# Attention values in full fp32, two heads in two 64-column tiles, and row sums added outside TensorE

## The chip, the cores and the metric

The kernel runs on one core of one Trainium2 chip. The metric is the time of one execution on the device in microseconds; the median over runs is compared.

## What is computed

One layer of a streaming encoder: a normalisation and one input projection, then three groups of heads on the projected columns (forgetting attention with 6 heads of 64, an RWKV-7 recurrence with 6 heads, cross-attention of 4 heads into 256 memory tokens), gates, one output projection and the residual. There are 2048 prompt tokens and eight sample streams of 16 tokens with 512 cached keys each; all is fp32. What the change touches is the softmax attention of the prompt, forgetting and memory:

```python
s = jnp.einsum('bqhd,bkhd->bhqk', q, k) * (HEAD_DIM ** -0.5)
s = s + jnp.transpose(cq, (0, 2, 1))[..., :, None] - jnp.transpose(ck, (0, 2, 1))[..., None, :]
s = jnp.where(kpos[None, :] <= qpos[:, None], s, jnp.finfo(jnp.float32).min)
p = jax.nn.softmax(s, axis=-1)
o = jnp.einsum('bhqk,bkhd->bqhd', p, v)
...
o = jnp.concatenate([o_f * jax.nn.silu(g_f), o_r * jax.nn.silu(g_r), o_m * jax.nn.silu(g_m)], axis=-1)
y = x + o @ w_out
```

## The kernel before

The program has two parts. The first, to about 1128 us, projects the input in four blocks of 512 tokens and runs the recurrence; queries, keys, values and gates go to DRAM. The second part holds the attention, the sample streams and the output projection.

Large products are done in a reduced-width form of fp32 (`F32R`): an operand is split into a high and a low part, and three matmuls (high-high, high-low, low-high) replace a full one. The splits are made by ScalarE (copy of the high part) and by GpSimd or VectorE (subtraction).

Attention works in units. A unit is a pair of heads `hp` (three pairs forgetting, two pairs memory) and a block of 512 queries `qb` (four). Forgetting units go over `4 * qb + 4` key tiles of 128, memory units over two. In the last four tiles of a forgetting unit the first columns are masked, so that widths of 512, 384, 256 and 128 queries remain. `queries` loads and splits the queries and takes row maxima from products of keys and queries (tile `pm`, reduced on VectorE). `attend` (from line 1138) does the rest, one key tile `kt` and one head `h` at a time, first all tiles of head 0, then of head 1:

- `scores` (line 1145): two matmuls into `pS` (two buffers), for masked tiles an addition on VectorE, the exponential on ScalarE into `P` (line 1154, two buffers), its high part `Ph` on ScalarE (line 1157), its low part `Pl` on GpSimd (`PLE`, line 61 of the helpers).
- `values` (line 1161), three steps (`LAG`) later: three matmuls into `po`, a PSUM tile of its own for each head with one buffer for forgetting units. The weights are the value tiles `vt` with a column of ones, 65 wide, so that row 64 of `po` is the row sum.
- at the last key tile three ScalarE copies take `po` to `ob` and the row sum; the row sums go to DRAM.
- `sums` (line 1204) reads them back as 32 x 32, takes reciprocals times 0.5, writes them to DRAM and reads them broadcast into `rb`; `out` multiplies `ob` by `rb` (VectorE) and by the gate (GpSimd) and stores it. The last forgetting unit has `ending` instead: one-row products spread the sums in `pd`.

`values_in` (line 1015) loads the values of 512 keys, fills `vt` with ones on GpSimd and splits the values on ScalarE and VectorE. `fox_keys` and `mem_keys` call it and make the split keys `K`.

Beside the forgetting units run memory units, sample streams and output projections (`py`, six to fifteen matmuls each, added on VectorE). The steps are emitted in a mix by their place in the sequence, and then `_arrange` orders all instructions of every engine anew: a list scheduler with a cost for each kind of instruction, due times and the buffers of each tile tries 18 orders and keeps the best by its own estimate. It takes neighbouring full fp32 matmuls that use less than the whole array as one unbroken run. It also knows which pools of the second part lie in the same SBUF bytes as pools of the first, and starts a tile only when those pools are done. The first keys `K` lie in pool `k0`, today in the bytes of pool `rw`; the pool behind that, `xs`, holds the normalised input `xk`.

## Time and profile before

| what | value |
|---|---|
| median of 3 runs | 1784.49 us (1782.93 to 1788.72) |
| span of the profiled execution, the only time given for it | 1786.9 us |
| granted TensorE clock, mean | 0.978 |
| HBM read, written | 210.15 MB, 90.28 MB |

The page has one line for the busy time of each engine. PE is TensorE's matmuls, PEld its weight loads, which run beside matmuls; DVE is VectorE, ACT ScalarE, POOL GpSimd, SP the queue that issues DMAs. The ends of matmuls are modelled, so that a matmul's duration includes about 0.17 us of the array's latency, which the next one overlaps: what a matmul costs in a stream is read from one start to the next. A full fp32 matmul stands in the trace as two records, a matmul in the reduced form as one. A row of a group gives the busy time in us, the mean in ns of one instruction, the engine's idle time before them and what ended it.

### The profile page before, as it was taken

How to read it: one execution, taken by the hardware profiler on the slowest of the kernel's cores; microseconds unless marked ns; L12 is line 12 of the kernel's file. 1: busy time of each engine (PE TensorE's matmuls, PEld its weight loads, DVE VectorE, ACT ScalarE, POOL GpSimd, SP SyncE). 2: the span in 40 equal slices, each digit the busy share in tenths (PEclk: the TensorE clock that was granted, in tenths of full speed). 3: DMA queues.
4: the chain of work that ended last, by engine and by line, in shares of the span. 5: the costliest groups of instructions: out<-in, count | busy, mean ns of one | idle time of the engine just before them, and what ended most of it. 6: DMA issues, size and time to landing. Idle time of an engine off the chain costs nothing.

```text
span 1786.9 us, 40906 instructions
## 1 busy us (share of the span) xinstructions
PE 1679.5 (94%) x16243; PEld 1347.0 (75%) x16243; DVE 980.2 (55%) x2310; ACT 897.2 (50%) x1783; POOL 808.7 (45%) x824
## 2 busy tenths in 40 slices
PE   4989999999899999999899999799999999989998
PEld 3989988787887688887688888576766666667776
DVE  6755554573444574345574372776545865676214
ACT  5434243434143523234323344688788777886552
POOL 4555452232312243132132143477687566766552
PEclk9999999999999999999899999799999899999999
DMA  7755764654645764655535654544445853344432
GB/s 207 276 185 174 224 196 143 206 188 137 201 143 150 245 194 145 193 167 176 169 113 166 190 169 154 156 127 139 156 149 172 271 207 110 103 152 158 155 111 107
DMA packets 236314, 303.11 MB, mean 170 GB/s; under 512 B 81594, under 2 KB 185976, under 8 KB 220250
## 3 DMA queue, kind: packets, MB, share of 16 engines
q1 hardware_dynamic: 236122, 300.49, 52.2%
q8 instruction: 128, 2.10, 0.5%
q14 instruction: 64, 0.52, 0.1%
HBM read 210.15 MB, written 90.28 MB: 168 GB/s over the span
## 4 chain that ended last, share of the span: by engine, by line
PE 51%; DMA 11%; DVE 6%; ACT 5%; POOL 3%; issue 2%; SPq 1%; DVEq 0%; POOLq 0%; ACTq 0%
PE pjd L58 12%; PE py L58 8%; PE po L58 7%; PE pjt L58 6%; PE pS L58 5%; PE pm L58 2%; DMA w<-w_d 1%; DMA xd<-inv_d 1%; POOL Pl L61 1%; PE sc L58 1%; ACT P L1154 1%; PE pz L58 1%; PE pa L58 1%; PE gr L58 1%; DMA AR<-sp_d 1%
## 5 line engine op out<-in xcount | busy, mean ns | idle before, releaser
L58 PE MATMUL pjd<-xk,w 128*128 128x512 f32 (+5 forms) x2280 | 537.8, 377 | 18.7 <-DMA w<-w_d 4.6
L58 PEld LDWEIGHTS pjd<-xk,w 128*128 128x128 f32 (+1 forms) x2280 | 385.8, 191 | 84.6 <-issue 7.8
L61 POOL TENSOR_TENSOR Pl<-P,Ph 128x512 fp32r<-128x512 f32 (+3 forms) x272 | 317.4, 1177 | 173.2 <-ACT Ph L1157 116.7
L58 PE MATMUL pjt<-w,xk 128*128 128x256 f32 x2040 | 295.5, 291 | 3.0 <-DVE xssg L64 1.7
L58 PEld LDWEIGHTS pjt<-w,xk 128*128 128x128 f32 x2040 | 267.8, 193 | 13.6 <-issue 3.9
L58 PE MATMUL py<-W,oh 128*128 128x512 f32 x816 | 239.1, 397 | 0.4 <-ACT Q L1126 0.2
L1154 ACT ACTIVATE P<-pS,NB 128x512 f32<-128x512 f32 x240 | 147.4, 623 | 88.8 <-PE pS L58 36.0
L58 PEld LDWEIGHTS py<-W,oh 128*128 128x128 f32 x816 | 149.9, 188 | 38.7 <-issue 0.8
L58 PE MATMUL pS<-Q,K 128*128 128x512 f32 (+1 forms) x480 | 154.7, 392 | 6.5 <-ACT P L1154 5.3
L58 PE MATMUL po<-Ph,vt 128*65 128x512 f32 x480 | 151.4, 370 | 4.2 <-ACT ob L1180 2.1
L1157 ACT CAST Ph<-P 128x512 fp32r<-128x512 f32 (+3 forms) x272 | 150.4, 565 | 9.1 <-PE po L58 4.5
L58 PEld LDWEIGHTS pS<-Q,K 128*128 128x128 f32 x480 | 85.5, 194 | 42.9 <-ACT P L1154 24.5
L1098 DVE TENSOR_REDUCE mx<-pm 128x1 f32<-128x512 f32 x144 | 95.2, 683 | 28.4 <-PE pm L58 27.3
L61 POOL TENSOR_TENSOR nr<-nr,mhalf 128x8 f32<-128x8 f32 (+2 forms) x43 | 61.7, 1435 | 98.7 <-DVE nr L67 89.2
L61 POOL TENSOR_TENSOR w<-wraw,w 128x1024 fp32r<-128x1024 f32 (+1 forms) x34 | 81.4, 2400 | 50.1 <-ACT w L202 44.8
L58 PE MATMUL pm<-K,Q 128*128 128x512 f32 (+3 forms) x240 | 92.8, 404 | 10.8 <-DVE mx L1095 5.2
L58 PE MATMUL po<-Pl,vt 128*65 128x512 f32 x240 | 89.1, 372 | 3.6 <-POOL Pl L61 3.5
L58 PEld LDWEIGHTS po<-Ph,vt 128*65 128x65 f32 x480 | 64.5, 137 | 33.2 <-ACT ob L1180 3.2
L61 DVE TENSOR_TENSOR xo<-py,xo 128x512 f32<-128x512 f32 x68 | 46.1, 686 | 75.3 <-PE py L58 74.9
L61 DVE TENSOR_TENSOR ytmp<-yt 64x14 f32<-64x14 f32 (+9 forms) x210 | 52.4, 249 | 42.0 <-DMA yt<-ld 37.4
L58 PEld LDWEIGHTS pm<-K,Q 128*128 128x128 f32 x240 | 47.2, 200 | 31.2 <-DVE mx L1095 7.9
L721 ACT COPY qk<-pjt 128x512 f32<-128x512 f32 (+1 forms) x47 | 26.1, 563 | 70.1 <-PE pjt L58 69.8
(404 smaller groups left out, 2820.0 us busy)
## 6 DMA issues: line engine op xcount, KB each, us to landing
w<-w_d SPq DMA_DIRECT2D x84, 1024.0 KB
w_d<-w SPq DMA_DIRECT2D x28, 1024.0 KB
y_d<-xo SPq DMA_DIRECT2D x21, 512.0 KB
wraw<-in_w_in SPq DMA_DIRECT2D x36, 256.0 KB
xo<-in_x SPq DMA_DIRECT2D x17, 512.0 KB
xo<-y_d SPq DMA_DIRECT2D x17, 512.0 KB
xt<-in_x SPq DMA_DIRECT2D x24, 256.0 KB
xraw<-in_xT SPq DMA_DIRECT2D x24, 256.0 KB
```

Source lines behind the costliest of these rows:

```text
L58: PE.matmul(out, lhsT, rhs, start=start, stop=stop, skip_group_check=True)
L61: e.tensor_tensor(out=out, in0=a, in1=b, op=op)
L721: S.copy(o_, out)
L1098: V.tensor_reduce(out=to, in_=pm[:, :n], op=MAX, axis=AX.X)
L1154: S.activation(P_[:, c0:], pS[:, c0:], AF.Exp, bias=NB[:, qb, 2 * hp + h, kt:kt + 1] if fox else 0.0)
L1157: S.copy(Ph[:, c0:], P_[:, c0:])
```

## The change

Values are kept in plain fp32 as they are loaded, without the column of ones and without a split. `P` is used as it is, also in fp32. Each head has one matmul per key tile, 64 columns wide; both heads write one `po`, head 0 in partitions 0 to 63 and head 1 in 64 to 127, and alternate. The steps are now groups of up to four key tiles of both heads (`GRP`); the values of a group are issued one group later (`LAG` = 1). `P` has 15 buffers, the tiles `Ph`, `Pl` and `rs` go. Row sums: from the second key tile on, GpSimd or VectorE adds `P` to a tile `z` for each head (two buffers for a pair), on VectorE for every third tile (`ZE`). `sums` then transposes `z` in blocks of 32 x 32, reduces it, adds across the four partition blocks with a matmul against a matrix of twos, and takes the reciprocal. One copy takes `po` to `ob`.

```diff
+ZE = "GGV"
-PMB, PSB, PB, HB, LB, LAG, NKB, BIG, POB, PTB = 2, 2, 2, 5, 5, 3, 4, 7, 1, 3
-PL = "G"
+PMB, PSB, PB, ZB, GRP, LAG, NKB, BIG, POB, PTB = 2, 2, 15, 2, 4, 1, 4, 7, 1, 3
...
+        twos = c2t("twos", [128, 128])
+        for j in range(4):
+            jj = slice(32 * j, 32 * j + 32)
+            ts(V, twos[jj].rearrange("p (a b) -> p a b", b=32), ident[jj, jj].unsqueeze(1).to_broadcast([32, 4, 32]), 2.0, None,
+               M, ALU.bypass)
...
-        def values_in(vt, vsrc, nt):
-            t_ = c2.tile([128, 4, 2, 64], F32, tag="tok", name="vtok", bufs=3)[:, :nt]
-            SY.dma_start(t_, vsrc.rearrange("(t p) (h d) -> p t h d", p=128, d=64))
-            G.memset(vt[:, 0:130 * nt].bitcast(F32), 1.0)
-            v1 = vt[:, 0:130 * nt].rearrange("p (t h d) -> p t h d", h=2, d=65)
-            v2 = vt[:, 130 * nt:258 * nt].rearrange("p (t h d) -> p t h d", h=2, d=64)
-            S.copy(v1[:, :, :, 0:64], t_)
-            tt(V, v2, t_, v1[:, :, :, 0:64].bitcast(F32), SUB)
-            return v1, v2
+        def values_in(vt, vsrc):
+            SY.dma_start(vt, vsrc.rearrange("(t p) (h d) -> p t h d", p=128, d=64))
+            return vt
...
-                vt = kp.tile([128, 1032], F32R, tag="vt", name="vt", bufs=NKB)
-                U["vt"].append(values_in(vt, v_d[gs, cs], 4))
+                vt = kp.tile([128, 4, 2, 64], F32, tag="vt", name="vt", bufs=NKB)
+                U["vt"].append(values_in(vt, v_d[gs, cs]))
...
-                P_ = lp.tile([128, 512], F32, tag="P", name="P", bufs=PB)
+                P_ = P[kt, h] = lp.tile([128, 512], F32, tag="P", name="P", bufs=PB)
                 S.activation(P_[:, c0:], pS[:, c0:], AF.Exp, bias=NB[:, qb, 2 * hp + h, kt:kt + 1] if fox else 0.0)
-                Ph = lp.tile([128, 512], F32R, tag="Ph", name="Ph", bufs=HB)
-                Pl = lp.tile([128, 512], F32R, tag="Pl", name="Pl", bufs=LB)
-                S.copy(Ph[:, c0:], P_[:, c0:])
-                tt(PLE[kt % len(PLE)], Pl[:, c0:], P_[:, c0:], Ph[:, c0:].bitcast(F32), SUB)
-                P[kt, h] = Ph, Pl
...
-                mm(po[h][0:65, c0:], v1, Ph[:, c0:], start=kt == 0, stop=False)
-                mm(po[h][0:64, c0:], v2, Ph[:, c0:], start=False, stop=False)
-                mm(po[h][0:65, c0:], v1, Pl[:, c0:], start=False, stop=kt == last - 1)
...
+                if kt == 1:
+                    if not h:
+                        R["z"] = lp.tile([128, 2, 512], F32, tag="z", name="z", bufs=ZB)
+                    if c0:
+                        G.tensor_copy(R["z"][:, h, :c0], P[0, h][:, :c0])
+                    tt(G, R["z"][:, h, c0:], P[0, h][:, c0:], P_[:, c0:], A_)
+                elif kt:
+                    tt(V if ZE[kt % len(ZE)] == "V" else G, R["z"][:, h, c0:], R["z"][:, h, c0:], P_[:, c0:], A_)
+
+            def values(kts):
+                if kts[0] == 0:
+                    R["po"] = (qc if fox else qa).tile([128, 512], F32, tag="po" if fox else "pt", name="po", bufs=POB if fox else PTB)
+                po = R["po"]
+                for kt in kts:
+                    c0 = c0_(kt)
+                    for h in range(2):
+                        mm(po[64 * h:64 * h + 64, c0:], U["vt"][kt // 4][:, kt % 4, h, :], P[kt, h][:, c0:],
+                           start=kt == 0, stop=kt == last - 1)
+                if kts[-1] == last - 1:
+                    R["ob"] = lt.tile([128, 512], F32, tag="ob", name="ob")
+                    S.copy(R["ob"], po)
+                    if dst is None:
+                        R["pd"] = qa.tile([128, 512], F32, tag="pt", bufs=PTB, name="pd")
+                        for h in range(2):
+                            mm(R["pd"][64 * h:64 * h + 64], one1.to_broadcast([128, 64]), R["z"][:, h])
...
             def sums():
+                rb = R["rb"] = lt.tile([128, 512], F32, tag="rb2", name="rb2", bufs=1)
+                zs = wk.tile([128, 32], F32, tag="zs", name="zs")
+                for h in range(2):
+                    V.transpose(rb, R["z"][:, h])
+                    V.tensor_reduce(out=zs[:, 16 * h:16 * h + 16], in_=rb.rearrange("p (a b) -> p a b", b=32), op=A_, axis=AX.X)
+                pz = qa.tile([128, 512], F32, tag="pt", bufs=PTB, name="pz")
+                mm(pz[:, 0:32], twos, zs)
+                rc = wk.tile([32, 2, 32], F32, tag="rc", name="rc")
+                V.reciprocal(rc[:, 0], pz[0:32, 0:32])
+                V.transpose(rc[:, 1], rc[:, 0])
                 rd = dt("rd", [2, 512], bufs=2)
-                rc = wk.tile([32, 32], F32, tag="rc", name="rc")
-                SY.dma_start(rc, R["sd"].rearrange("h (a b) -> (h a) b", b=32))
-                V.reciprocal(rc, rc)
-                ts(V, rc, rc, 0.5, None, M, ALU.bypass)
-                SY.dma_start(rd.rearrange("h (a b) -> (h a) b", b=32), rc)
-                R["rb"] = lt.tile([128, 512], F32, tag="rb2", name="rb2", bufs=1)
+                SY.dma_start(rd.rearrange("h (a b) -> (h a) b", b=32), rc[:, 1])
```

## Rows read from the trace of the kernel before

**Rows 1.** The page: its first line and part 1, the busy time of each engine with its share of the span and its instructions.

```profile
span 1786.9 us, 40906 instructions
...
PE 1679.5 (94%) x16243; PEld 1347.0 (75%) x16243; DVE 980.2 (55%) x2310; ACT 897.2 (50%) x1783; POOL 808.7 (45%) x824
```

**Rows 2.** Busy time of each engine in four stretches of the second part (start and end, length; then PE, PEld, DVE, ACT and POOL with their instructions, the granted clock, the DMA engines' share and GB/s).

```profile
1128.00:1179.00 51.00, 42.07 (x171) 29.04 (x171) 45.48 (x103) 39.46 (x77) 26.98 (x35) 0.77 0.52 165
1179.00:1382.00 203.00, 197.15 (x942) 141.02 (x940) 118.60 (x238) 170.57 (x310) 157.19 (x152) 1.00 0.46 145
1382.00:1585.00 203.00, 190.10 (x1379) 129.85 (x1380) 137.06 (x354) 163.97 (x318) 135.08 (x143) 0.96 0.51 172
1585.00:1787.00 202.00, 193.29 (x870) 144.75 (x868) 82.48 (x146) 99.36 (x172) 105.87 (x91) 1.00 0.39 136
```

**Rows 3.** Groups of PE from 1128 us to the end, different shapes apart: one of the three value matmuls of each step by its width, and the small full fp32 products of the sample units (two records each).

```profile
L58 PE MATMUL po<-Pl,vt 128*65 128x512 f32 x168 | 68.2, 406 | 1.8 <-POOL Pl L61 1.8
...
L58 PE MATMUL po<-Pl,Km 128*65 128x512 f32 x32 | 12.7, 396 | 1.0 <-POOL Pl L61 1.0
...
L58 PE MATMUL po<-Pl,vt 128*65 128x384 f32 x24 | 8.4, 348 | 1.7 <-POOL Pl L61 1.7
...
L58 PE MATMUL po<-Pl,vt 128*65 128x256 f32 x24 | 7.0, 292 | 0.0
L58 PE MATMUL po<-Pl,vt 128*65 128x128 f32 x24 | 5.7, 239 | 0.1
...
L58 PE MATMUL pN<-sD,one 128*128 128x128 f32 x12 | 3.1, 341 | 0.0
```

**Rows 4.** Timeline of PE near 1170 us (start, length of the merged piece, count): the three value matmuls of one step and what follows.

```profile
1169.79 0.62 PE L58 MATMUL po<-Ph,vt 128*65 128x512 f32 x2
1170.25 0.39 PE L58 MATMUL po<-Pl,vt 128*65 128x512 f32 x1
1170.48 0.40 PE L58 MATMUL pr<-idr,turnm 128*64 128x128 f32 x4
```

**Rows 5.** Timelines of PE: four full fp32 products in four 32-column tiles of the array in a sample unit, first in a window that holds the first four of their eight records only, then in one that holds all; then two such products in two 64-column tiles with 128 moving columns.

```profile
1432.69 0.40 PE L58 MATMUL pm<-K,Q 128*128 128x512 f32 x1
1433.02 0.64 PE L58 MATMUL pS<-sB,sD 128*32 128x512 f32 x4
...
1433.02 1.06 PE L58 MATMUL pS<-sB,sD 128*32 128x512 f32 x8
1434.02 0.50 PE L58 MATMUL pS<-Q,K 128*128 128x512 f32 x1
...
1417.68 0.44 PE L58 MATMUL po<-sD,sC 128*64 128x128 f32 x4 [0.23 <-ACT sD L1301]
```

**Rows 6.** Groups of ScalarE over the whole span: the copies of `P`, the exponentials of forgetting units, and one of the three closing copies.

```profile
L1157 ACT CAST Ph<-P 128x512 fp32r<-128x512 f32 (+3 forms) x272 | 150.4, 565 | 9.1 <-PE po L58 4.5
L1154 ACT ACTIVATE P<-pS,NB 128x512 f32<-128x512 f32 x240 | 147.4, 623 | 88.8 <-PE pS L58 36.0 <-DVE pS L61 32.9 <-POOL Pl L61 13.6
...
L1177 ACT COPY ob<-po 64x512 f32<-64x512 f32 x20 | 11.5, 578 | 0.4
```

**Rows 7.** Groups of GpSimd from 1128 us to the end, different shapes apart: the subtractions.

```profile
L61 POOL TENSOR_TENSOR Pl<-P,Ph 128x512 fp32r<-128x512 f32 x200 | 261.3, 1317 | 108.2 <-ACT Ph L1157 76.4 <-issue 14.1 <-PE pm L58 6.9
...
L61 POOL TENSOR_TENSOR Pl<-P,Ph 128x384 fp32r<-128x384 f32 x24 | 25.6, 1067 | 27.0 <-ACT Ph L1157 12.5 <-DMA y_d<-xo 5.4 <-PE po L58 3.5
...
L61 POOL TENSOR_TENSOR Pl<-P,Ph 128x256 fp32r<-128x256 f32 x24 | 18.1, 756 | 14.8 <-ACT Ph L1157 13.9 <-POOL Qm L1083 0.7
L61 POOL TENSOR_TENSOR Pl<-P,Ph 128x128 fp32r<-128x128 f32 x24 | 13.2, 548 | 23.2 <-ACT Ph L1157 13.9 <-PE pm L58 3.3 <-PE pS L58 3.1
```

**Rows 8.** Who waited for whom from 1140 us to the end (us in total, times, longest us): PE and its weight loads behind the exponential and behind the subtraction.

```profile
PEld pS L58 <- ACT P L1154: 29.3, 72, 1.8
...
PEld po L58 <- POOL Pl L61: 8.4, 13, 1.8
...
PE pS L58 <- ACT P L1154: 6.1, 11, 1.5
...
PE po L58 <- POOL Pl L61: 4.5, 5, 1.5
```

**Rows 9.** Instructions on the keys `K` and on the normalised input `xk` (duration in ns at least, median and at most; first and last start), and the first product of keys on PE's timeline.

```profile
L1004 POOL MEMSET K<- x24: 519/520/523, 1119.1 to 1612.0; 64x512 f32 x24
...
L58 PE MATMUL pjd<-xk,w x2280: 274/389/798, 19.2 to 1125.1; 128*128 128x512 f32 x105, 128*128 128x256 f32 x41, 128*128 128x384 f32 x32, 128*70 128x512 f32 x8
...
1126.64 0.30 PE L58 MATMUL pm<-K,Q 128*128 128x128 f32 x1 [1.13 <-POOL vt L1018]
```

**Rows 10.** VectorE: groups from 1128 us to the end (a maximum, an addition with one operand in PSUM, a product of two SBUF operands, the subtraction for the values, the scaling of the reciprocals), and the transposes of 128 x 256 at line 479 of the first part.

```profile
L1098 DVE TENSOR_REDUCE mx<-pm 128x1 f32<-128x512 f32 x144 | 95.2, 683 | 28.4 <-PE pm L58 27.3
L61 DVE TENSOR_TENSOR xo<-py,xo 128x512 f32<-128x512 f32 x68 | 46.1, 686 | 75.3 <-PE py L58 74.9
...
L61 DVE TENSOR_TENSOR ob<-ob,rb 128x512 f32<-128x512 f32 x19 | 17.4, 918 | 19.2 <-DMA rb<-rd 16.7 <-DMA ot<-o_d 2.0 <-issue 0.4
...
L61 DVE TENSOR_TENSOR vt<-vtok,vt 128x512 fp32r<-128x512 f32 x12 | 9.0, 751 | 4.8 <-ACT vt L1021 4.8
...
L67 DVE TENSOR_SCALAR rc<-rc 32x32 f32<-32x32 f32 x19 | 8.6, 452 | 0.4
...
L479 DVE STREAM_TRANSPOSE x<-xd x12: 445/446/447, 124.5 to 1079.3; 128x256 f32<-128x256 f32 x12
```

**Rows 11.** Busy time in the third stretch of the instructions on `Pl` alone (PE, PEld, POOL with their counts, clock, DMA share, GB/s).

```profile
1382.00:1585.00 203.00, 36.36 (x96) 13.39 (x96) 109.41 (x97) 0.96 0.51 172
```

More of the change, by code (lines that the diff above doesn't have):

```diff
@@ L979 @@
         taken = [0, 0]
-        PLE = [{"V": V, "G": G}[x] for x in PL]
         cl = lt.tile([48, 512], F32, tag="ob", name="cl")
@@ L1050, in step @@
                 m = big("Km", F32R)
[L1051 removed]
+                vt = m[:, 1024:1280].bitcast(F32).rearrange("p (t h d) -> p t h d", h=2, d=64)
+                U["vt"] = [values_in(vt, mv_d[:, cs])]
                 pt = turned_in(mk_d[:, cs], 256)
@@ L1140, in attend @@
             last = 4 * qb + 4 if fox else 2
-            seq = [(kt, h) for h in range(2) for kt in range(last)]
-            P, po, R = {}, {}, {}
+            P, R = {}, {}
             c0_ = lambda kt: 128 * max(0, kt - 4 * qb) if fox else 0
@@ L1189, in step @@
+            groups = [list(range(k, min(k + GRP, last))) for k in range(0, last, GRP)]
             def step(i):
-                if i < len(seq):
-                    scores(*seq[i])
+                if i < len(groups):
+                    for kt in groups[i]:
+                        for h in range(2):
+                            scores(kt, h)
                 if i >= LAG:
-                    values(*seq[i - LAG])
+                    values(groups[i - LAG])
             def ending():
@@ L1220, in out @@
                 SY.dma_start(dst, R["ob"])
-            return [lambda i=i: step(i) for i in range(len(seq) + LAG)], [ending] if dst is None else [sums, out]
+            return [lambda i=i: step(i) for i in range(len(groups) + LAG)], [ending] if dst is None else [sums, out]
         def sample(fox, hp):
```

27 lines of the change are left out of this document (2 added, 25 removed).

## The prediction

> **What bounds the kernel now.** I read the page first: PE is busy for 94% of the span, the other engines for about half [rows 1]. Such a mean says little about one stage, so I cut the part in which the attention runs into four stretches [rows 2]. The changed code runs from about 1128 us to the end. In that part PE is busy for 622.6 of 659 us (the four PE columns added), the granted clock is 0.96 to 1.00 after 1179 us, and the next engine changes place: ScalarE (171 of 203 us) and GpSimd (157) in the second stretch, VectorE (137), ScalarE (164) and GpSimd (135) in the third, nobody in the fourth. TensorE bounds it, with little room between its instructions. What the change does to TensorE's work is then the main term, and what it puts on VectorE in the third stretch the main doubt.
>
> **The values on TensorE (removed and added).** Today each key tile of each head takes three matmuls: high values with high weights, low with high, high with low. The counts by width [rows 3] give the work: 200 key-tile-and-head steps of 512 columns (168 + 32), 24 each of 384, 256 and 128; in units of 512 columns 200 + 18 + 12 + 6 = 236. Three such matmuls start at 1169.79 us and the next instruction starts at 1170.48 [rows 4]: 0.69 us, 0.23 each. So 236 x 0.69 = 163 us.
>
> The new form issues one full fp32 matmul per step, two heads in the two column halves of the array. The trace has this kind twice. In the sample units four 32-column fp32 matmuls of 512 columns stand side by side: eight records, two per matmul; the first four end 0.64 us after the start, all eight after 1.06 [rows 5], so one round of all column tiles is 0.42 us and a matmul two rounds, whichever number stands beside it. With 64 columns, as here, there is only a shorter case of 128 moving columns: four records, two matmuls, in 0.44 us together [rows 5]. I take 0.43 a round, 0.86 for a pair of heads: 118 x 0.86 = 101 us. Going into another tile shape costs too: the matmul before that run starts at 1432.69 and needs 0.23, the next after it starts at 1434.02, so the run took 1.10 us of which two rounds are 0.86: 0.24 us per run [rows 5]. Groups are up to four key tiles: 1 + 2 + 3 + 4 per head pair, three pairs, plus eight memory units: 38 runs, 9 us. New total 110 us. **Term 1: 110 - 163 = -53 us**, on PE, which is the path.
>
> The Trainium skill says in TensorE: Matmul & The Clock Gate, section "Measured speedup vs the span model", that three column tiles of 32 gave 2.38 times, not 3. By that efficiency (0.79) the pairs would be an estimated 101 / 0.79 = 128 us instead of 101, and the time 1766. The trace's four tiles, at one common round of 0.42 us, show no such loss; a partial loss has its place under the rivals.
>
> **The row sums.** The ones column goes, and with it two row-sum copies' worth of work per unit. GpSimd and VectorE add the exponentials in z instead; at the end of 19 of the 20 units VectorE transposes and reduces z twice and one 32-column fp32 matmul adds across partitions and doubles. That matmul's nearest row is six 128-column fp32 products in 3.1 us, 0.5 us each [rows 3]; with a quarter of the columns I bound it by 0.2 and 0.5, so 4 to 10 us. **Term 2: +5 us.** The last unit's column of ones against z replaces two one-row products of the same width: nothing either way, its z is added while PE has output projections queued.
>
> **ScalarE and GpSimd.** ScalarE loses the 272 copies of P (150 us) and two of three closing copies of 0.58 us in 20 units (23 us) [rows 6]. GpSimd loses its 272 subtractions (261 + 26 + 18 + 13 = 318 us) [rows 7]. In return GpSimd gets, by the order G, G, V over key tiles from the second on, 112 adds of 512 columns, 18 of 384, 12 of 256 and 18 of 128 and six small copies; at the durations of its present two-operand forms (1.32, 1.07, 0.76, 0.55) that is 148 + 19 + 9 + 10 + 3 = 189 us. Both engines are off the path and get lighter, by 173 and 129 us. That is worth what PE waits for them: weight loads and matmuls of pS waited 29.3 + 6.1 us for the exponential, those of po 8.4 + 4.5 us for the subtraction [rows 8], 48 us in all. A weight load's wait runs partly beside a matmul still in flight; the matmuls' own idle time is 6.1 + 4.5 = 11 us. So between 0 and -48; I take near the lower row, **term 3: -12 us**. Late next behind a pS buffer is the exponential itself, which stays.
>
> **Waiting for a group.** A run needs all eight exponentials of its group at once; today a step needs one. If each of 38 runs waited for one more exponential, at 0.61 us (147.4 us over 240 [rows 6]), that is 23 us; if the other work in PE's queue (output projections, maxima) always covers it, 0. While a run of 3.4 us goes on, maxima and projections stand behind it in PE's queue, and VectorE and ScalarE, which drain them, run dry after two buffers each. The planner orders by such costs, so I take the lower part, **term 4: +5 us**.
>
> **Where the attention starts.** The three new or larger small tiles take 512 + 256 + 256 bytes a partition below the first key tiles. By the declared sizes those tiles end 352 bytes short of the pool of the normalised input today; afterwards they reach 672 bytes into it, and must wait until its last product. K is first written at 1119.1 us, the last product of xk starts at 1125.1 [rows 9]: at most 6 us later. But the first product of K starts at 1126.64 anyway, behind GpSimd's fill of vt, which goes [rows 9]. Between 0 and 6.5, **term 5: +3 us**.
>
> **VectorE.** It gets 72 adds (48 of 512 columns, 6 of 384, 12 of 256, 6 of 128). Its row with two SBUF operands beside a busy GpSimd is ob, 0.92 us, against 0.69 with one operand in PSUM [rows 10]: 44 + 4 + 7 + 2 = 57 us. Two transposes and two reductions close each of 19 units: the transpose of 256 columns takes 0.445, so 0.89 for 512, the reduction 0.68 [rows 10]: 60 us. Gone are the subtraction for vt (9 us) and the scaling of the reciprocals (about 9). Net +100 us. In the third stretch, which has 97 of the 272 steps [rows 11], about 20 us of adds and 25 of closings come to 137: 182 of 203 us. If PE's work there shrinks by its share of term 1 (18 us), VectorE would be at 98%: it can't all be taken. I charge a third of the 18, **term 6: +6 us**, and 0 elsewhere, where VectorE stays under 80% (119 + 42 of 203; 82 + 29 of 202). The cover is that PE's queue holds projections while VectorE adds; if it is gone, up to 100 us are exposed.
>
> On the queues: three small DMAs per unit (two row sums out, one back) leave SP; the value tiles are now loaded straight into vt, so a load may hold those behind it on SP until that buffer is free, while four buffers as today keep this rare. I cost it at nothing.
>
> **Sum.** 1786.9 - 53 + 5 - 12 + 5 + 3 + 6 = 1740.9 us. The profiled execution's span is 2.4 us over the median of the runs (1784.49) and inside their spread, so the median should be 2.4 lower: 1738.5, I say **1739**.
>
> **The rivals.** (a) PE's waits were ScalarE's and GpSimd's doing all along, and go almost whole: term 3 becomes -40, and time 1711. For it: both are at 77 to 84% of the second stretch [rows 2]. Against: the fourth stretch has them at half and PE is no fuller there (96%, against 97% in the second). (b) **Slower: VectorE takes the path.** In place of the removed waits comes one for VectorE, which now drains maxima and projections late because each add holds it 0.92 us or more and each closing 3.1 us. With all of the 100 us on the path instead of 6 the time is 1739 + 94 = 1833; it comes out slower than now once about half of the 100 is exposed. For it: the third stretch at 98%. Against: it had 40% spare in the rest, and GpSimd, which blocks it, is used 129 us less. The Trainium skill has the mechanism in SBUF — State Buffer, section "SBUF: two separate sides": an op of VectorE with two SBUF inputs and a GpSimd op lock one port pair for each other's whole instruction; by that rule z's adds, on both engines, collide with each other. The ob row agrees (0.92 against 0.69). (c) The change doesn't do what it says: the two halves don't run side by side. Then the steps cost 236 x 0.86 + 9 = 212 us, +49 instead of -53, and the time is 1841. A partial loss, a quarter of the way from 101 to 203, would be 126 + 9 us and make it 1764. Against both: the start of all four tiles within one round [rows 5].
>
> **How the numbers follow.** My forecast with its terms 0.70; (a) 0.14; (b) 0.12, spread evenly: 0.04 between 1755 and 1779, 0.04 within 0.3% of now, 0.04 above; (c) 0.04, half of it the partial loss and faster, half slower. About 5 us (0.3%) is what a measurement of this kernel can tell from no change. Faster 0.70 + 0.14 + 0.04 + 0.02 = 0.90, same 0.04, slower 0.06. The range: with term 3 near its far end and terms 4 and 5 at zero, 1786.9 - 53 + 4 - 40 + 6 - 2.4 = 1702; with term 2 at 10, term 3 at 0, term 4 at 23, term 5 at 6.5 and term 6 as taken, 1777. I give these two as the range.
>
> **What would show it.** Right: value matmuls in pairs a few ns apart, a run of eight 3.4 to 3.7 us long, their total near 110 us; ScalarE near 300 us and GpSimd near 295 us in the attention part; PE still over 93% busy there. Wrong: pairs one behind the other; PE's idle time ended by VectorE's adds, transposes or maxima; a first product of K several us later after the last of xk. The prediction fails most easily if VectorE fills the third stretch.

## The result and the profile after

The change takes 1766.38 us (median of 4 runs, 1759.87 to 1769.24) against 1786.61 for the kernel before beside it: ratio 0.988, 95% interval [0.985, 0.992]. It is faster by 20 us; 45 were forecast. The profiled execution has a span of 1762.2 us.

The page's first line and engine line, to set beside [rows 1]:

```profile
span 1762.2 us, 39877 instructions
...
PE 1639.0 (93%) x16009; PEld 1277.3 (72%) x16009; DVE 1053.2 (60%) x2448; ACT 727.2 (41%) x1457; POOL 677.6 (38%) x704
```

ScalarE and GpSimd do what the sum had them do (305 and 290 us after 1128 us); VectorE has 460 us there, 76 more than before, where the sum had 100 more. To see where the time went I cut both kernels at the same work, not at the same time: at the last score of a memory unit and at the last product of the sample units with their cached values. Between the two lies the stretch of the sample units, which has hardly any output projections in it (15 of the change's 816 `py` matmuls). The first window begins at 1128 us in both. Windows of the kernel before (start and end, length; PE, PEld, DVE, ACT and POOL busy, granted clock, DMA share, GB/s):

```profile
1128.00:1383.00 255.00, 240.18 (x1117) 170.81 (x1116) 164.53 (x342) 211.01 (x388) 185.05 (x188) 0.95 0.47 150
1383.00:1539.50 156.50, 147.12 (x1173) 99.86 (x1171) 107.02 (x277) 123.44 (x242) 99.90 (x105) 0.95 0.56 190
1539.50:1786.90 247.40, 235.31 (x1077) 174.00 (x1073) 112.07 (x222) 138.92 (x247) 140.18 (x128) 1.00 0.39 130
```

The same of the kernel after:

```profile
1128.00:1365.00 237.00, 221.55 (x1029) 143.98 (x1030) 195.53 (x401) 138.56 (x247) 122.57 (x131) 0.94 0.49 161
1365.00:1531.80 166.80, 148.01 (x1121) 87.70 (x1119) 125.84 (x305) 82.90 (x159) 72.12 (x78) 0.90 0.52 176
1531.80:1762.20 230.40, 216.89 (x983) 150.89 (x979) 138.52 (x268) 83.93 (x143) 95.57 (x89) 0.99 0.41 137
```

The stretches ahead and behind gain 18 and 17 us. The middle one loses 10, although TensorE has less to do there. PE stands idle for 18.8 us in it (166.8 - 148.0; before 9.4), and the granted clock is 0.90, which is 33 us at the lower level (166.8 x 2 x 0.10); before 0.95 of 156.5, 16 us. VectorE is busy for 75% of it: it is not full.

Added up over the three windows, PE is busy for 586.4 us, where it was 622.6, and idle for 47.8, where it was 36.3. TensorE's work thus falls by 36 us (terms 1 and 2 have 48), and its idle time rises by 11.5 (terms 3 to 6 have 2). By the clocks above some 25 us more than before are at the lower level (66 against 41), and they cost at most half of that. So the 21 us that this execution lacks against the sum (1762.2 against 1740.9) are about 12 of slower work and 9.5 of idle time.

The attention also starts later behind the first part. The last product of `xk` starts at 1122.4 us (1125.1 before [rows 9]), the first key tile is written right behind it, and PE stands idle for 5.40 us before its first product with keys, where it was 1.13:

```profile
L58 PE MATMUL pjd<-xk,w x2280: 274/389/803, 14.9 to 1122.4; 128*128 128x512 f32 x109, 128*128 128x256 f32 x42, 128*128 128x384 f32 x31, 128*70 128x512 f32 x4
...
L1009 POOL MEMSET K<- x24: 520/520/752, 1122.9 to 1572.5; 64x512 f32 x24
...
1128.66 0.77 PE L58 MATMUL pS<-Q,K 128*128 128x512 f32 x1 [5.40 <-issue]
```

The values themselves are as forecast. PE's timeline around one run at the full clock:

```profile
1450.74 0.72 PE L58 MATMUL pS<-Q,K 128*128 128x512 f32 x2 [0.29 <-ACT P L1153]
1451.39 3.65 PE L58 MATMUL po<-P,vt 128*64 128x512 f32 x16
1454.98 1.21 PE L58 MATMUL pS<-Q,K 128*128 128x512 f32 x4
```

Eight pairs of records, 3.59 us to the next start: 0.43 a round and 0.15 at the end. The largest group of value matmuls and pz (busy, mean ns, idle before them):

```profile
L58 PE MATMUL po<-P,vt 128*64 128x512 f32 x336 | 80.9, 615 | 0.0
...
L58 PE MATMUL pz<-zs,twos 128*128 128x32 f32 x38 | 7.0, 268 | 1.6 <-DVE zs L1205 1.5
```

The runs wait for nothing (0.0). The waits are at the scores, and they grew; the lines that answer to [rows 8]:

```profile
PEld pS L58 <- ACT P L1153: 35.4, 74, 1.8
...
PE pS L58 <- ACT P L1153: 12.6, 22, 1.5
```

How such a wait comes about is seen at 1377 to 1383 us. VectorE's timeline:

```profile
1377.19 1.14 DVE L61 TENSOR_TENSOR ob<-ob,rb 128x512 f32<-128x512 f32 x1
1378.26 0.29 DVE L61 TENSOR_TENSOR pS<-pS,negm 128x128 f32<-128x128 f32 x1
1378.46 0.70 DVE L1204 STREAM_TRANSPOSE rb<-z 128x512 f32<-128x512 f32 x1
1379.08 0.93 DVE L61 TENSOR_TENSOR z<-z,P 128x256 f32<-128x256 f32 x1
1379.94 0.67 DVE L1205 TENSOR_REDUCE zs<-rb 128x16 f32<-128x512 f32 x1
1380.54 0.28 DVE L61 TENSOR_TENSOR pS<-pS,negm 128x128 f32<-128x128 f32 x1
```

and TensorE's beside it:

```profile
1377.43 0.44 PE L58 MATMUL pm<-K,Q 128*128 128x512 f32 x1
1379.41 0.44 PE L58 MATMUL pS<-Q,K 128*128 128x128 f32 x2 [1.53 <-ACT P L1153]
1381.28 0.80 PE L58 MATMUL pS<-Q,K 128*128 128x512 f32 x1 [1.43 <-ACT P L1153]
1382.78 0.61 PE L58 MATMUL pz<-zs,twos 128*128 128x32 f32 x2 [0.71 <-DVE zs L1205]
```

These are masked scores at the end of a unit. A score goes from PE to a mask addition on VectorE, to the exponential, and only then is its pS buffer free. The mask addition of 1378.26 stands behind a product, the one of 1380.54 behind a transpose, an addition and a reduction of row sums; PE waits 1.53, 1.43 and 0.71 us in 5. The closing has a part in two of these waits: its reduction holds the second mask addition up by some 0.6 us, and the 0.71 are pz's. Then the clock falls. Windows before and from 1381 us, and the same at the next masked group:

```profile
1415.00:1422.00 7.00, 4.14 (x23) 2.63 (x25) 6.31 (x18) 3.42 (x7) 2.72 (x5) 0.98 0.98 376
1422.00:1429.00 7.00, 7.00 (x25) 2.60 (x26) 5.12 (x12) 0.37 (x1) 1.29 (x3) 0.51 0.92 325
...
1374.00:1381.00 7.00, 4.01 (x26) 3.19 (x24) 7.00 (x17) 4.04 (x9) 4.07 (x5) 1.00 0.97 290
1381.00:1388.00 7.00, 6.02 (x18) 2.65 (x20) 6.83 (x20) 1.37 (x4) 1.89 (x4) 0.51 0.94 334
```

In both places PE was busy for 4 of 7 us with VectorE at 6.3 and 7.0, and in the next 7 us the granted clock is 0.51, the level of 1.2 GHz. What follows such waits then runs at half speed as well. But waits are not behind every fall. In the same stretch the clock also falls at 1412 and at 1446 us, and in the 7 us ahead of either TensorE was busy all the time; most of the records there are the 128 products of 16 columns at the end of a sample unit's values. The kernel before has two falls in the same place, at 1422 and 1456 us. The first of the change's two:

```profile
1405.00:1412.00 7.00, 7.00 (x146) 5.22 (x143) 5.49 (x12) 2.22 (x5) 4.62 (x5) 0.99 0.24 68
1412.00:1415.30 3.30, 3.30 (x12) 2.55 (x11) 2.28 (x8) 0.69 (x1) 1.86 (x3) 0.50 0.76 251
```

### The profile page after: what moved, and what is told of

Same layout as the page of the kernel before. It is cut to its first block, busy times and chain, and to the rows that moved or that the text cites. A ratio compares the mean times of both kernels' runs of the same rounds, so it can differ in the third digit from the quotient of the medians.

```text
span 1762.2 us, 39877 instructions
## 1 busy us (share of the span) xinstructions
PE 1639.0 (93%) x16009; PEld 1277.3 (72%) x16009; DVE 1053.2 (60%) x2448; ACT 727.2 (41%) x1457; POOL 677.6 (38%) x704
## 5 line engine op out<-in xcount | busy, mean ns | idle before, releaser
L58 PEld LDWEIGHTS pjd<-xk,w 128*128 128x128 f32 (+1 forms) x2280 | 380.2, 189 | 89.0 <-DVE xk L61 9.3
L58 PE MATMUL py<-W,oh 128*128 128x512 f32 x816 | 231.9, 399 | 1.1 <-DVE xo L61 0.6
L1153 ACT ACTIVATE P<-pS,NB 128x512 f32<-128x512 f32 (+1 forms) x240 | 144.4, 624 | 131.0 <-DVE pS L61 64.6
L58 PE MATMUL pS<-Q,K 128*128 128x512 f32 (+1 forms) x480 | 157.8, 405 | 20.1 <-ACT P L1153 12.6
L61 POOL TENSOR_TENSOR z<-z,P 128x512 f32<-128x512 f32 (+3 forms) x120 | 136.2, 1147 | 99.2 <-ACT P L1153 76.8
L58 PE MATMUL pm<-K,Q 128*128 128x512 f32 (+3 forms) x240 | 98.6, 430 | 10.0 <-DVE mx L1098 4.6
L58 PE MATMUL po<-P,vt 128*64 128x512 f32 (+1 forms) x480 | 98.5, 555 | 0.0
L61 POOL TENSOR_TENSOR oh<-ot,oh 128x384 fp32r<-128x384 f32 (+2 forms) x38 | 43.8, 1153 | 108.4 <-ACT oh L1361 80.6
L58 PEld LDWEIGHTS pm<-K,Q 128*128 128x128 f32 x240 | 47.8, 204 | 39.1 <-DVE mx L1098 14.2
L61 POOL TENSOR_TENSOR z<-P 128x512 f32<-128x512 f32 (+1 forms) x40 | 49.7, 1256 | 68.7 <-ACT P L1153 68.4
L58 PEld LDWEIGHTS po<-P,vt 128*64 128x64 f32 x480 | 33.2, 143 | 56.2 <-issue 54.5
L61 DVE TENSOR_TENSOR z<-z,P 128x512 f32<-128x512 f32 (+3 forms) x72 | 63.0, 880 | 16.6 <-POOL z L61 8.0
```

Of the source, the lines that this page charges most:

```text
L58: PE.matmul(out, lhsT, rhs, start=start, stop=stop, skip_group_check=True)
L61: e.tensor_tensor(out=out, in0=a, in1=b, op=op)
L1153: S.activation(P_[:, c0:], pS[:, c0:], AF.Exp, bias=NB[:, qb, 2 * hp + h, kt:kt + 1] if fox else 0.0)
```

## Experiments

Eighteen kernels ran, each with the kernel before beside it (medians 1784 to 1790). Ratios below are to that; 0.001 is 1.8 us.

**Additions, groups, all row sums, first keys.** First I took VectorE's filled queue (theory V) against the long groups (theory G).

```diff
-ZE = "GGV"
+ZE = "G"
```

> All additions to z go to GpSimd; VectorE loses 72 additions (63 us of its busy time after the change). The changed kernel stands at 1766 us, some 27 us over the forecast, and the loss lies in the sample stretch. Theory V (VectorE's additions hold up maxima and masks that PE waits for): 1750 to 1756 us, ratio about 0.981. Theory G (a group's unbroken run of eight value matmuls, which needs eight exponentials and leaves PE without other work where no output projections are queued): 1763 to 1770 us, ratio 0.987 to 0.991.

1765.12 us, 0.990 [0.987, 0.993]: no gain; theory V fails. The additions on VectorE, alone, are not what costs.

```diff
-PMB, PSB, PB, ZB, GRP, LAG, NKB, BIG, POB, PTB = 2, 2, 15, 2, 4, 1, 4, 7, 1, 3
+PMB, PSB, PB, ZB, GRP, LAG, NKB, BIG, POB, PTB = 2, 2, 15, 2, 2, 1, 4, 7, 1, 3
```

> Groups of two key tiles instead of four, so a run is four matmuls long (1.75 us) and needs four exponentials; 68 runs instead of 38, which costs 30 x 0.24 = 7 us of PE. Theory G: the waiting halves, -13 to -20 us, against +7: 1753 to 1760 us, ratio about 0.983. Theory V: only the 7 us, 1770 to 1775 us, ratio about 0.992.

1783.38 us, 0.998 [0.996, 1.000]: slower than the change by 17 us, which neither theory had. Up to 30 more runs (68, not 38) at 0.24 us of tile change would explain 7, and in the profiled execution 15 us lie in the first part of the program, which the edit does not touch (see the table under the order). Theory G had 6 to 13 us less, so long groups are not shown to cost anything; G falls.

```diff
+                if dst is not None:
+                    pass
-                if kt == 1:
+                elif kt == 1:
...
-                for h in range(2):
-                    V.transpose(rb, R["z"][:, h])
-                    V.tensor_reduce(out=zs[:, 16 * h:16 * h + 16], in_=rb.rearrange("p (a b) -> p a b", b=32), op=A_, axis=AX.X)
...
-                mm(pz[:, 0:32], twos, zs)
...
-                V.reciprocal(rc[:, 0], pz[0:32, 0:32])
-                V.transpose(rc[:, 1], rc[:, 0])
+                V.memset(rc[:, 1], 1.0)
```

> Leaves out the row sums of 19 of 20 units: no additions to z, no transposes, reductions and matmul against twos; the reciprocals are a constant one (the output is not normalised there). VectorE loses about 120 us, GpSimd 165 us. Theory V: the whole shortfall comes back, 1735 to 1742 us, ratio about 0.974. Theory G: PE's 6 us and little more, 1755 to 1762 us, ratio about 0.984.

1747.96 us, 0.980 [0.977, 0.982]: without the row sums the kernel is 18 us faster, between the two theories.

```diff
-        twos = c2t("twos", [128, 128])
+        twos = kp.tile([128, 128], F32, tag="twos", name="twos")
...
-                zs = wk.tile([128, 32], F32, tag="zs", name="zs")
+                zs = wk.tile([128, 32], F32, tag="zs", name="zs", bufs=1)
...
-                rc = wk.tile([32, 2, 32], F32, tag="rc", name="rc")
+                rc = wk.tile([32, 2, 32], F32, tag="rc", name="rc", bufs=1)
```

> The matrix of twos lies in a later pool and the two small sums tiles have one buffer, so that the first key tiles again end short of the pool of the normalised input. If they cost the start of the attention something (term 5 of the forecast, 0 to 6.5 us), 1760 to 1765 us; theories G and V both expect no more than that: 1762 to 1768 us, ratio 0.985 to 0.989.

1770.79 us, 0.992 [0.988, 0.995]: no gain in the whole time, and above the numbers of both theories. In the trace the first product with keys starts at 1126.2 us, even before the last one of `xk` (1126.8), so the wait of 5.40 us is gone; what it is worth is smaller than what moves the time from kernel to kernel.

**Closings or additions; samples or not; more pS.** The third diff without its first lines, so that the additions stay:

```diff
-                for h in range(2):
-                    V.transpose(rb, R["z"][:, h])
...
-                V.transpose(rc[:, 1], rc[:, 0])
+                V.memset(rc[:, 1], 1.0)
```

> Leaves out the closings of the row sums (transposes, reductions, the matmul against twos; the reciprocal is a constant one), keeps all additions; the output is not normalised. With the additions too it was 18 us under the change (1748). Theory C, the closings are what costs: on VectorE they are 52 us in short bursts that stand in front of mask additions and maxima; 1748 to 1752 again. Theory A, the additions cost, by holding P and z and by keeping GpSimd busy: 1762 to 1767, like the change.

1746.21 us, 0.978 [0.974, 0.981]. Theory C holds: leaving the closings out gains all that leaving out the row sums gained, and the additions cost nothing that shows. Its windows, cut like those above:

```profile
1128.00:1364.00 236.00, 221.99 (x1042) 149.49 (x1041) 165.29 (x355) 143.88 (x258) 127.93 (x142) 0.93 0.54 172
1364.00:1509.00 145.00, 133.24 (x1101) 80.37 (x1101) 111.52 (x280) 83.48 (x162) 66.04 (x75) 0.99 0.58 202
1509.00:1736.90 227.90, 217.63 (x986) 150.40 (x982) 123.81 (x243) 84.11 (x143) 99.30 (x92) 0.99 0.40 138
```

This is the main reading of the study. The stretch of the samples is 22 us shorter: 7 of idle time (11.8 for 18.8), and the clock is at 0.99, so that some 3 us there are at the lower level and not 33. Thirty such microseconds fewer save at most 15: 7 + 15 = 22. This profile is of the fastest of the four executions (1738.7 us, mean clock 0.980; the others 0.967 to 0.972), but the kernel without any row sums has as short a stretch:

```profile
1375.00:1517.10 142.10, 132.48 (x1087) 79.57 (x1085) 87.88 (x253) 80.40 (x158) 17.70 (x32) 0.96 0.60 206
```

The stretches ahead and behind look nearly as long as in the change (236 and 237, 228 and 230), but the first window begins at a fixed time, and in this kernel the first part ends later: its last product of `xk` starts at 1133.7 us, in the change at 1122.4. Counted from there the first stretch is 12 us shorter too (230.3 and 242.6). Of the 19 closings 11 stand in the first stretch, four in that of the samples and four in the last (38 reductions at line 1205, 22, 8 and 8 of them). So the closings cost in the first stretch as well, only less for each.

The edit takes out more than work. The constant reciprocals wait for no sums: they are all sent off by 1211 us, in the change by 1665, unit by unit (first this kernel, then the change):

```profile
L1203 DVE MEMSET rc<- x19: 85/85/85, 1116.2 to 1210.8; 32x32 f32 x19
...
L1209 DVE RECIPROCAL rc<-pz x19: 334/341/346, 1165.6 to 1663.8; 32x32 f32<-32x32 f32 x19
```

So the chain from the sums to the product goes with the closings, and this run can't tell the two apart.

Nor are the waits at masked scores the bulk of the difference. PE's idle time behind the exponential in the stretch of the samples, in the change and without closings (us, times, longest):

```profile
PE pS L58 <- ACT P L1153: 7.9, 12, 1.5
...
PE pS L58 <- ACT P L1153: 6.7, 10, 1.5
```

Only 1.2 of the 7 us of idle time are there; the rest is spread over many short waits, mostly for VectorE and for the sample units' own steps.

```diff
             r = [load]
-            for h in range(2):
-                r += [lambda f=f, h=h: f(h) for f in (masked, soft, turn)]
-            return r + [values, out]
+            return [gate, out]
```

(`gate` loads the gates, and `out` stores them as they are.)

> The change with the work of the five sample units left out (their output rows are the gates). Read against the kernel before with the same left out. Theory S, the missing gain is lost in the stretch of the sample units, where no output projections are left to fill TensorE's waits: without them the change is worth 40 us or more, as forecast. Theory B, the gain is lost wherever forgetting units run, at scores that come in groups: without the samples it is still worth about 20 us.

> The kernel before with the work of the five sample units left out: the control of the run above. Its time is no test by itself; the difference of the two is: 40 us or more by theory S, about 20 us by theory B.

1714.89 and 1752.78 us: without the sample units the change is worth 37.9 us, just under the 40 of theory S and nearly twice the 20 of theory B.

```diff
-PMB, PSB, PB, ZB, GRP, LAG, NKB, BIG, POB, PTB = 2, 2, 15, 2, 4, 1, 4, 7, 1, 3
+PMB, PSB, PB, ZB, GRP, LAG, NKB, BIG, POB, PTB = 2, 3, 15, 2, 4, 1, 4, 7, 1, 2
```

> Three buffers for pS and two for the shared PSUM tiles pt, in place of two and three. Theory B, a group's eight scores in a row wait for the two pS buffers, since an exponential takes 0.69 us and a score 0.46: the third buffer takes most of the 23 us of waits before scores away, 1748 to 1758. Theory S: the waits only move to the tiles pt, 1764 or more.

1800.4 us, 1.007 [1.004, 1.009]. A miss for both: 34 us slower than the change. The kernel's PSUM pools hold eight tiles of this size (two pm, two pS, one po, three pt), and the edit takes the third pS from pt; the weight loads' waits behind maxima grew (17.6 us, 14.5 in the change), and 17 of the 35 us lie in the first part (table below). It doesn't clear the two pS buffers of blame.

**The halves of the closings.**

```diff
-                pz = qa.tile([128, 512], F32, tag="pt", bufs=PTB, name="pz")
-                mm(pz[:, 0:32], twos, zs)
...
-                V.reciprocal(rc[:, 0], pz[0:32, 0:32])
+                V.reciprocal(rc[:, 0], zs[0:32])
```

> Closings without the matmul against twos and without its shared PSUM tile: VectorE transposes and reduces as in the change, and takes the reciprocal of its own partial sums (the four partition blocks are not added). The closings cost 20 us (1766 with them, 1746 without). Theory V, their cost is VectorE's 52 us of transposes and reductions in front of other work: 1760 to 1767, little gained. Theory P, their cost is the PSUM tile and TensorE's wait for the sums: 1746 to 1752.

```diff
-                for h in range(2):
-                    V.transpose(rb, R["z"][:, h])
-                    V.tensor_reduce(out=zs[:, 16 * h:16 * h + 16], in_=rb.rearrange("p (a b) -> p a b", b=32), op=A_, axis=AX.X)
...
-                mm(pz[:, 0:32], twos, zs)
+                for h in range(2):
+                    mm(pz[:, 0:32], one1.to_broadcast([128, 128]), R["z"][:, h, 0:32], start=not h, stop=h == 1)
```

> The other half: no transposes and reductions on VectorE, but a shared PSUM tile and two small matmuls per unit that read the sums z (32 columns of each head against ones, in place of one matmul against twos; the output is not normalised rightly). Theory V: 1746 to 1752. Theory P: 1760 to 1767.

1755.07 us, 0.980 [0.974, 0.987], and 1763.94 us, 0.986 [0.981, 0.990]. The first is halfway between the two theories, the second at P; both intervals reach to the change's. Their windows over the stretch of the samples (from the last memory score to the last sample product; first without pz, then without the transposes and reductions):

```profile
1363.00:1530.00 167.00, 149.07 (x1118) 88.88 (x1118) 130.16 (x308) 85.62 (x164) 70.99 (x79) 0.92 0.52 178
```

```profile
1362.00:1526.00 164.00, 149.71 (x1117) 90.85 (x1115) 117.91 (x291) 85.19 (x163) 73.91 (x80) 0.90 0.54 185
```

167 and 164 us at clocks of 0.92 and 0.90: either half alone leaves the stretch long and the clock low. Neither V nor P alone is shown; the 145 us came only with both gone. In both kernels PE's idle time behind the exponential fell, from the change's 7.9 us, and the stretch stayed as long, which speaks against the masked scores as the cause:

```profile
PE pS L58 <- ACT P L1153: 3.2, 8, 0.9
...
PE pS L58 <- ACT P L1153: 2.4, 7, 0.8
```

What both halves keep, and the kernels without closings lack, is a reciprocal that waits for the sums. That this wait costs, and not the work of either half, would fit all of these runs; none tests it.

Then the edit of the samples and that of the closings in one kernel:

> The change without the work of the sample units and without the closings. Without samples the change was 37.9 us faster than before without them, 18 more than with them. Theory O (one cause), the closings cost what they cost because they meet the sample units on VectorE: no further gain, 1708 to 1716. Theory T (two causes), closings cost wherever they stand: 20 us less again, 1692 to 1698.

1703.08 us: against the kernel before without samples the ratios differ by 0.9807 - 0.9519 = 0.029, 51 us. Between theories O and T. The closings cost 12 us here (13 by the ratios), so less than with the samples, but they cost where there are no samples too. The forecast without its terms for the closings (2 and 6) has 56 us.

**Closings by another way.**

```diff
-                    V.transpose(rb, R["z"][:, h])
-                    V.tensor_reduce(out=zs[:, 16 * h:16 * h + 16], in_=rb.rearrange("p (a b) -> p a b", b=32), op=A_, axis=AX.X)
...
+                for h in range(2):
+                    mm(pz[64 * h:64 * h + 64], one1.to_broadcast([128, 64]), R["z"][:, h])
+                S.copy(rb, pz)
+                for h in range(2):
+                    SY.dma_start(sd[h:h + 1], rb[64 * h:64 * h + 1])
+                rc = wk.tile([32, 32], F32, tag="rc", name="rc")
+                SY.dma_start(rc, sd.rearrange("h (a b) -> (h a) b", b=32))
+                V.reciprocal(rc, rc)
+                ts(V, rc, rc, 0.5, None, M, ALU.bypass)
```

> Closings by another way, complete: two full fp32 matmuls of 512 columns against ones (two 64-column tiles side by side, 0.43 us a unit and up to 0.27 for the change of tile shape), one ScalarE copy, and the DMAs through DRAM that the kernel before had, so that VectorE has only a reciprocal of 32 x 32 and a product. Takes some 50 us from VectorE and gives TensorE 8 to 13 us. Theory V: 1754 to 1760, faster than the change. Theory P: 1766 to 1780, since the PSUM tile is held longer.

1838.18 us, 1.026 [1.021, 1.032]. A clear miss: 72 us slower than the change (67 by the ratios), where 14 at most were expected. TensorE's own work is larger than I had it: a pair of matmuls is two rounds, 0.86 us and not 0.43, and the sums keep PE busy for 19.9 us, not 8 to 13. Some 31 us lie in the first part (table below). VectorE has 33 us less to do than in the change, and it doesn't help. The mean granted clock is 0.947 over the run. On its PE timeline a run of value matmuls over a masked group (widths 512, 384, 256 and 128; the merged line names the first alone) takes 4.46 us to the next start. The same kind of run at the full clock takes 2.30 (at 1232.15 us; the next start is 1234.45):

```profile
1190.51 4.54 PE L58 MATMUL po<-P,vt 128*64 128x512 f32 x16
1194.97 1.17 PE L58 MATMUL pm<-Km,Qm 128*128 128x256 f32 x4
...
1232.15 2.38 PE L58 MATMUL po<-P,vt 128*64 128x512 f32 x16
1234.45 0.50 PE L58 MATMUL pm<-K,Q 128*128 128x512 f32 x1
```

The window around the first has PE busy for 6.66 of 7 us at a clock of 0.51:

```profile
1189.00:1196.00 7.00, 6.66 (x24) 2.98 (x22) 3.74 (x9) 4.63 (x9) 1.74 (x4) 0.51 0.02 4
```

Why this order lost so much more than its work isn't settled.

**The order.** How much of such differences is the order that the scheduler happens to find?

```diff
-_TRIES = ((0.3, 0), (0.45, 0), (0.6, 0))
+_TRIES = ((0.35, 0), (0.5, 0), (0.65, 0))
```

> The change, with the same instructions in another order: the list scheduler starts its attempts from weights of 0.35, 0.5 and 0.65 in place of 0.3, 0.45 and 0.6. Theory R, part of the missing gain is the order that the scheduler found for this kernel: the time moves by 8 us or more either way. Rival: the cause is in the work and its waits, and the time stays within 4 us of the change, 1762 to 1770.

> The same for the kernel before. Theory R: it moves by 8 us or more too, 1778 or less or 1795 or more. Rival: within 4 us of 1786.

After 1780.11 us, 0.995 [0.992, 0.998]; before 1796.73, 1.003 [1.001, 1.005]. The same instructions in another order cost the change 11.5 us (0.0064) and the kernel before 5. Theory R holds for the change. The kernel before, at 1796.73, is past the 1795 that theory R named, but only 5 to 7 us above the kernel before beside it (1790.09). The gain between the two stays at 17 us. Differences under some 10 us between single kernels above (the halves of the closings) are therefore not told from order. The 18 to 20 us without closings were seen in two kernels.

The profiles show where much of this scatter lies: in the first part, which the change and the experiments leave as it is. In every kernel it has the same 2280 products of `xk`, but the last of them starts between 1118.5 and 1153.7 us. The time from there to the end of the same execution compares the second part alone:

| kernel | last product of `xk`, us | from there to the end, us |
|---|---|---|
| before; the change | 1125.1; 1122.4 | 661.8; 639.8 |
| additions on GpSimd | 1121.6 | 642.0 |
| groups of two | 1137.7 | 638.2 |
| keys clear | 1126.8 | 634.2 |
| no row sums | 1141.1 | 601.3 |
| no closings | 1133.7 | 603.2 |
| without pz; without transposes and reductions | 1126.4; 1122.9 | 631.6; 638.4 |
| three pS; sums by matmul | 1139.2; 1153.7 | 658.4; 682.8 |
| no samples: before; the change; no closings | 1127.2; 1118.5; 1129.0 | 624.5; 595.9; 571.5 |
| other order: before; the change | 1139.1; 1141.1 | 661.0; 647.6 |
| samples spread: before; the change; other order; no closings | 1152.9; 1128.8; 1136.0; 1139.7 | 664.5; 629.8; 628.3; 613.5 |

By this measure, of one execution each, the change gains 22 us; another order moves the change by 8 and the kernel before by 1. Without closings the second part is 37 us shorter, without any row sums 38, without the samples 24. The whole times show less of it because the first part of these kernels took 10 to 19 us longer; why, no run shows.

Then the sample units over a longer stretch, alone, in the kernel before, in the other order and without closings:

```diff
-X0, X3, X1, X2 = 0.02, 0.35, 0.6, 0.8
+X0, X3, X1, X2 = 0.02, 0.35, 0.7, 0.84
```

> The change, with the sample units emitted over a longer stretch (to 0.7 of the forgetting units' sequence, not 0.6) and the projections behind them to 0.84, not 0.8. Theory S, a stretch full of sample units with no projections as filler loses 15 us: with the units spread more thinly each waits beside more work, 1750 to 1760. Rival: it is no matter of density, and the projections that come later are missed earlier, 1764 to 1775.

> The same for the kernel before, where the stretch of the samples had TensorE busy 141 of 150 us: little to win, 1780 to 1790 by either theory; the gap to the run with the change is what is read, 30 us or more by theory S, about 20 by its rival.

> The samples spread out, in an order from the other weights (0.35, 0.5, 0.65), which cost the change 11 us. Theory S, the density of the sample units decides: 1752 to 1764 again, 12 us or more under the change in that order (1780). Theory R, the faster time with the samples spread out was the luck of one order: 1768 to 1785.

> The samples spread out as in the faster run (1758) and the closings left out (the output is not normalised). Theory T, closings cost by themselves: about 20 us less than with them, 1734 to 1742. Theory O, what they cost was their meeting with the samples or the order found: 1746 to 1758.

The change 1758.15 us, 0.982 [0.979, 0.986]; the kernel before 1815.23, 1.012 [1.008, 1.016]. The second is a miss, 25 us over the 1790 at most that either theory had, so the gap of 57 us says little about the change: by the table 28 of the 30 us that this profiled execution is longer lie in the first part. In the other order 1766.43, 0.990 [0.986, 0.994], 14 us under the change in that order by the medians and 8 by the ratios. So the spread version was faster in both orders, by 8 to 14 us, as theory S had it, though the second time lies above its upper number; each of the two differences is about as large as what order alone did. Without the closings too, 1751.26 us, 0.981 [0.977, 0.984]: only 7 us less by the medians and 3 by the ratios; the 20 us of the closings do not return in this mix (theory O), though by the table the second part is 16 us shorter. Here the clock stays low without closings as well. The stretch of the samples, spread out, with and without them:

```profile
1369.00:1544.60 175.60, 159.52 (x1190) 94.37 (x1190) 140.40 (x351) 95.72 (x185) 80.73 (x93) 0.92 0.52 176
...
1375.00:1546.00 171.00, 158.21 (x1183) 94.18 (x1181) 125.24 (x314) 95.81 (x186) 80.58 (x93) 0.90 0.52 178
```

So the low clock of the change's stretch is not the closings' doing alone. The spread version has the lowest time of the complete kernels, some 32 us under the kernel before beside it; its interval overlaps that of the change.

## Why the prediction was right in direction and wrong in size

- **Term 1 (-53) was right.** Side by side at 0.43 us a round, with 0.15 us behind a run of eight; rival (c) falls. From the start of each value run to the next start PE has 111 us in all, 110 were forecast. The efficiency of 0.79 that I estimated beside it from the Trainium skill (TensorE: Matmul & The Clock Gate, "Measured speedup vs the span model") isn't seen in two 64-column tiles: records of a pair are one round, as above. That its 1766 is the time measured is chance; the missing time is not in the value runs.
- **Term 2 (+5)**: 7.0 us busy for pz. Sized rightly.
- **Term 3 (-12) failed.** The waits behind the subtraction are gone (4.5 + 8.4 [rows 8]), but those behind the exponential rose by as much (6.1 + 29.3 to 12.6 + 35.4; without closings 10.2 + 30.3). A step's scores used to have 0.69 us of value matmuls between them; now they stand together, and the chain through mask addition, exponential and pS is in the open. That the masked tiles are the place is read from one timeline; a kernel without mask additions wasn't tried on the chip.
- **Term 4 (+5)**: the runs wait 0.0. The groups make their wait at the scores, not at the values, and smaller groups were no faster.
- **Term 5 (+3)** was undersized: the first key tile is written 0.5 us behind the start of the last product of `xk`, where it was 6 us ahead of it, and the first product with keys starts 6.3 us behind it, 1.5 before. That is 5 us, near the far end of its bounds. The kernel with the keys clear has a second part 5.6 us shorter, but no lower time.
- **Term 6 (+6) is the step that failed most.** I charged VectorE's new work by how full it makes the third stretch, and a third of the room. VectorE got less than I had (76 us net, the transposes 0.70 and not 0.89) and was at 75% in the stretch of the samples; I had 98% for the third stretch. Yet with its closings left out the kernel was 18 to 20 us faster (12 without the samples, 3 to 7 with the samples spread out), and the second part of the profiled execution 37 us shorter; terms 2 and 6 together had 11. What a closing costs is not told by the engine's mean share. How it costs stays open: a closing in front of mask additions is seen on the timeline, but waits at scores are 1.2 of the 7 us of idle time that the stretch of the samples loses without closings, and neither half of a closing alone brings the stretch back.
- **The sum had no term for the clock.** Some 25 us more than before at the lower level are up to 12 of the 21 us that the profiled execution lacks. The forecast took the clock of the kernel before as given.
- The cover that I named for VectorE ("PE's queue holds projections") fits what the runs show, since the sample units lack it and the change is worth 38 us without them, not 20 (29 and 22 in the second part alone, by the table); each of these is of one order. Rival (b) had the place right and may have the engine right (the run without transposes and reductions, 52 us less on VectorE, was no faster in that stretch); the range of 1755 to 1779 that I gave a 0.04 is where the time fell. The shared port of the Trainium skill (SBUF — State Buffer, "SBUF: two separate sides") agrees with the additions of 512 columns, 1.03 us each (49.3 us for 48) against 0.69 with one operand in PSUM [rows 10], but they are not what costs: all of them on GpSimd gave the same time.

Not settled: which part of a closing matters (VectorE's bursts, pz's PSUM tile, the wait of the reciprocals for the sums, or the DRAM round trip that VectorE waits for, 15.1 us in all, 16.7 before). Either half alone left the stretch long, and what order alone does is as large as most of the differences. That the clock, and not something that comes with it, makes the 15 us is worked out from windows; no run held the clock fixed, and what brings it down is not shown. That the time lies inside the range is luck in part: its upper end came from terms 2 to 5, and what used it up was term 6 and the clock.

## What to carry to other kernels

Look first at how long the part takes that an edit does not touch: here it moved by up to 35 us between kernels, more than the change itself. Cut both traces at the same work, at both ends of a stretch, and compare there. New work on a side engine is not priced by the engine's mean share; ask what stands behind it in that queue and what waits for its result. An experiment that leaves work out also leaves out the waits for its result, so keep one version that does the waiting without the work. And before a difference of half a per cent is credited to an edit, give the same instructions another order.

## What the runs showed of the hardware

The 32 x 32 block transpose of 128 x 512 on VectorE took 0.70 us, not the 0.89 that two transposes of 256 columns would [rows 10]. A full fp32 value run of eight steps of 512 columns took 3.59 us to the next start at the full clock. A run over a masked group took 2.30 us at the full clock and 4.46 in a window at 0.51 (sums by matmul). The mean granted clock of the profiled executions lay between 0.947 (sums by matmul) and 0.980 (no closings) with nearly the same products, and within the four executions of one kernel (no closings) between 0.967 and 0.980.
